# The first MLP's down projection in seven products, and the conditioning spread over TensorE and VectorE

## The chip, the cores and the metric

The kernel runs on one core of a Trainium2 chip: TensorE (PE) for matrix products, VectorE (DVE), ScalarE (ACT), GpSimd (POOL), and SyncE (SP), which issues all DMAs of this kernel in one queue. The metric is the device time of one execution in microseconds.

## The reference

One step of a two-layer encoder over 1024 prompt and 32 sample tokens, 1056 columns in the kernel. Everything is float32. What matters here:

```
D_MODEL = 1024; D_FF = 4096; DEPTH = 2
sh1, sc1, g1, sh2, sc2, g2 = split(silu(c) @ w_ada[l] + b_ada[l], 6)     # per layer, two conditions
kv_shift, kv_scale = split(silu(c) @ w_ada_kv + b_ada_kv, 2)
u = x * (1 + sc1) + sh1
y = mlstm(u) @ w_out_a            # layer 0;  layer 1: chunk-band attention @ w_out_b
x = layer_norm(ALPHA * x + (1 + g1) * y)
u = x * (1 + sc2) + sh2
f = square(relu(u @ w_up[l])) @ w_down[l]
x = layer_norm(ALPHA * x + (1 + g2) * f)
```

`c` has two rows, one for the prompt and one for the sample, so each conditioning vector is a product of a 1024 x 1024 matrix with two columns. Layer 0 needs six such vectors at the beginning. Layer 1 needs six and the shared K/V two, 64 column groups of 128.

## The kernel before

Activations lie transposed: 128 features on the partitions, tokens along the row. Tokens are cut into three blocks `TBS` of 384, 384 and 288, or into quarters `QN` of 264, two of which make a pair. For float32 accuracy each operand is split into a high and a low part (`split`: a cast on ACT and a subtraction on DVE), and each product is three matmuls, high x high, high x low and low x high (`proj`, L118 to L120). Weights come as 0.5 MB tiles (`wblock`): a DMA into one of three `raw` buffers, then a split into one of six `wc` buffers.

The order of the stages is: layer 0's conditioning and mixer, its output projection (`out_proj`, "op_a"), the first MLP, Q, K and V projections, attention, output projection ("op_b"), the second MLP, output.

A framework turns the program order into the order of each engine and places the waits. In between stands `Flow`: a generator such as a LayerNorm (`norm`) or the conditioning is added to it, each finished tile calls `flow.tick(us)`, and the generator goes on one step when the ticks that it asked for are used up. `flow.finish` issues the rest at once.

**First MLP, `mlp` (L1006).** 8 groups of 512 hidden features. `up(g, c, ti)` makes 128 of them for one block of tokens: 24 matmuls, relu and square on ACT, the split on DVE into `hs`. `down(g, w, fc, ...)` makes 12 matmuls for 128 outputs of one block and DVE adds them, times the gate, to the accumulator (`add_gated_at`, L986). Up of the next group alternates with down of this one. In the last group the blocks are finished one by one, with some up tiles between the first and the second, and `end0` starts the LayerNorm of each.

**Second MLP, `mlp7` (L1124).** Hidden features go in 16 blocks of 256. Up runs first, over everything. For the first 14 blocks (`NW`), four tiles (two halves of the features by two quarters) fill one `H` (3 buffers); ACT squares them, DVE forms sums and differences, and seven operands are split into `HL` (1 buffer) and stored to DRAM (`hd`, L1170). Blocks 14 and 15 are `up_plain`. Then down runs as a seven-product scheme (Strassen's, in Winograd's form): `forms` builds the seven weight operands from two raw tiles, `unit` does the seven products for one of 4 groups of blocks and one of 4 column groups, in an order of TensorE that is written out by hand, and `fill` brings the stored operands back into free `rooms`, among them the space of the inputs that up no longer needs. `step` and `prep` prepare the weights two units ahead. The two plain blocks follow as an ordinary product.

**Conditioning.** Layer 0's first two parts are done on TensorE at the start (`ada_mm`, L380): the condition is the weight operand, 32 columns wide, and the rows of the matrix stream through into a strip of 32 PSUM rows; four strips are used. All else is done on DVE (`ada_cols`, L225): for two column groups, 8 row blocks x 2 conditions of scalar times tile plus accumulator, 256 wide (L238, L241), then a transpose and a sum (L245, L246), and after four such pairs a small product on TensorE (L252). `ada_rest` (L1382) runs layer 1's 48 and the 16 column groups of K/V in this way beside the first MLP, starting at its third block, and `end0` finishes it before the last LayerNorms. Its tiles take turns with the weights in the three `raw` buffers.

Of the kernel before, what the change touches and what calls it, by code (L numbers as in the profile page):

```python
# [15 lines left out]
P = 128  # L16
# [59 lines left out]
def trunk_kernel(ctx: ExitStack, tc: tile.TileContext, a, o):  # L76
# [148 lines left out]
    def ada_cols(src, c0, base, nch, mk, tmp_f, step, raw_f=raw_tile):  # L225

        for j in range(0, nch, 2):
# [21 lines left out]
            if j // 2 % 4 == 3:  # L249
                ps = mk(f"adas_{base}_{j}")  # L250
                for q in range(4):
# [7 lines left out]
                    op=ALU.add)  # L259

# [539 lines left out]
    def open_acc(l, order, between=None):  # L800

        cms, accs = {}, {}
        for ti in reversed(order):
            cms[ti] = tc.tile_pool(name=f"acc{l}_{ti}", bufs=1, side="right", reuse_waits="tile")
            accs[ti] = cms[ti].__enter__().tile([P, KC, TBS[ti][1]], F32, name=f"acc{l}_{ti}")
        for ti in order if between is None else reversed(order):
            t0, n = TBS[ti]
            nc.sync.dma_start(accs[ti], xsp[l][:, :, t0:t0 + n])
            if between:
                between(ti)  # L810
        return cms, accs

    ADA_B = (4.0, 2.0, 1.0)
    NOW = True
    TAIL = (1.0, 1.5)
    W00 = (6.0, 12.0, 0.0, 0.0, 0.0, 3.0)
    W01 = (6.0, 12.0, 3.0, 3.0, 3.0)
    W10 = ((10.0, 12.0, 0.0, 0.0, 0.0, 3.0), (16.0, 14.0, 0.0, 0.0, 0.0, 3.0))
    EARLY = 2

    def make_layer(acc, pp, uo, cut=None):
# [184 lines left out]
        def mlp(hp, l, gate, order, before_tb, after_tb, last):  # L1006
            w_up, w_dn = a["w_up"][l], a["w_down"][l]
            NG = 8
            hs = {}
            wups = {}  # L1010

            def up_w(g, pr):
                if (g, pr) not in wups:
                    wups[g, pr] = [wblock(f"up{l}_{g}_{pr}_{i}", w_up, 512 * i, g * 512 + pr * 256) for i in range(2)]
                return wups[g, pr]

            def up(g, c, ti):
                t0, n = TBS[ti]
                ps = mm(f"up_{l}_{g}_{c}_{t0}")
                proj(ps[:, :n], n, up_w(g, c // 2), c % 2, lambda hl, k: uo(hl, k, t0, n))  # L1020
                if (g, c) not in hs:
                    hs[g, c] = hp.tile([P, 2, T], F32R, tag="h", name=f"h_{l}_{g}_{c}", bufs=5)
                ht = hs[g, c]
                r = tmp_t([P, 384], f"r_{l}_{g}_{c}_{t0}")[:, :n]
                nc.scalar.activation(r, ps[:, :n], AF.Relu)  # L1025
                nc.scalar.activation(ht[:, 0, t0:t0 + n], r, AF.Square)
                nc.vector.tensor_mul(r, r, r)
                nc.vector.tensor_sub(ht[:, 1, t0:t0 + n], r, ht[:, 0, t0:t0 + n].bitcast(F32))  # L1028
                flow.tick(n / 96)
# [769 lines left out]
```

## Time and profile before

| | us |
|---|---|
| median of 3 runs | 2479.54 (2476.41 to 2479.93) |
| profiled execution, device time | 2479.81 |
| its span, first to last instruction | 2478.0 |
| TensorE busy / VectorE busy / ScalarE busy | 2413.7 / 1759.7 / 1016.9 |
| first up matmul of the first MLP | 515.1 |
| first Q matmul | 1263.6 |
| first up matmul of the second MLP | 1732.2 |
| its first down matmul | 2110.2 |

The granted TensorE clock is 0.992 on average over the span. A row of the timeline has the start, the duration and the instruction; successive matmuls overlap, so their pace is the distance of their starts. A row of a group has the line, the engine, the operation, result and operands, shapes and count, then the busy time, the mean duration in ns, and the idle time before. A row of stages has the bounds, the length, then busy time and count of PE, weight loads, DVE, ACT and POOL, the clock, the DMA share and GB/s. In square brackets stands for how long an engine was idle before an instruction and what ended this.

### The profile page before, as it was taken

The numbers are of one execution on the slowest core, as the hardware profiler recorded it, in microseconds if no ns is written. First come the engines' busy times: TensorE is split into PE (matmuls) and PEld (weight loads), VectorE is DVE, ScalarE is ACT, GpSimd is POOL, SyncE is SP. The second block draws the span as 40 slices with busy tenths as digits, with TensorE's granted clock in tenths as the row PEclk, the third lists the DMA queues.
The fourth block names the chain that finished last, engine by engine and source line by source line (L and its number), as shares of the span: only waits on it lengthen the run. The fifth ranks groups of instructions, "written<-read, shape, count | busy, mean of one in ns | idle before, by whom it ended". The sixth has DMA issues, their size and how long they took to land.

```text
span 2478.0 us, 42688 instructions
## 1 busy us (share of the span) xinstructions
PE 2413.7 (97%) x16844; PEld 2315.4 (93%) x16844; DVE 1759.7 (71%) x4038; ACT 1016.9 (41%) x2118; POOL 168.6 (7%) x315
## 2 busy tenths in 40 slices
PE   7999999999999999999999999999999999999997
PEld 4999999999999999999999867789999999899997
DVE  4899999788679679677597667746853442776758
ACT  4644456382211212212266556654754443221212
POOL 0211100000000000000001134410000000000003
PEclk9999999999999999999999989999999999999999
DMA  8433224313224224234122310050375646767632
GB/s 297 122 110 101 84 88 129 107 35 119 77 87 137 84 86 135 80 92 142 43 98 82 91 40 1 18 147 27 134 251 212 215 179 254 262 239 273 255 130 72
DMA packets 236220, 318.10 MB, mean 128 GB/s; under 512 B 11624, under 2 KB 185084, under 8 KB 234996
## 3 DMA queue, kind: packets, MB, share of 16 engines
q1 hardware_dynamic: 236020, 315.38, 38.8%
q8 instruction: 132, 2.16, 0.4%
q14 instruction: 68, 0.56, 0.1%
HBM read 242.79 MB, written 74.91 MB: 128 GB/s over the span
## 4 chain that ended last, share of the span: by engine, by line
PE 78%; DVE 8%; DMA 6%; ACT 2%; issue 1%; POOL 0%; SPq 0%; DVEq 0%; POOLq 0%; ACTq 0%
PE up L118 10%; PE up L120 10%; PE up L119 9%; PE dn L1283 9%; PE dn L119 5%; PE dn L118 5%; PE dn L120 5%; DMA fx<-hd 3%; PE pv L1608 2%; PE pt L1588 2%; PE s L1558 2%; PE o L118 1%; PE o L119 1%; PE o L120 1%; PE op_b L118 1%
## 5 line engine op out<-in xcount | busy, mean ns | idle before, releaser
L120 PE MATMUL up<-u,w_up 128*128 128x264 f32 x1024 | 292.9, 286 | 0.0
L118 PE MATMUL up<-u,w_up 128*128 128x264 f32 x1024 | 292.4, 286 | 0.0
L119 PE MATMUL up<-u,w_up 128*128 128x264 f32 x1024 | 291.1, 284 | 0.0
L1283 PE MATMUL dn<-fx,wf 128*128 128x264 f32 x2208 | 275.3, 286 | 7.9 <-DMA fx<-hd 7.4
L1283 PEld LDWEIGHTS dn<-fx,wf 128*128 128x128 f32 x2208 | 272.2, 189 | 9.7 <-issue 4.6
L119 PE MATMUL dn<-h,w_dn 128*128 128x384 f32 (+1 forms) x768 | 249.5, 325 | 0.0
L118 PE MATMUL up<-U,w_up 128*128 128x384 f32 (+1 forms) x768 | 249.2, 324 | 0.0
L119 PE MATMUL up<-U,w_up 128*128 128x384 f32 (+1 forms) x768 | 247.9, 323 | 0.0
L118 PE MATMUL dn<-h,w_dn 128*128 128x384 f32 (+1 forms) x768 | 247.8, 323 | 0.0
L120 PE MATMUL up<-U,w_up 128*128 128x384 f32 (+1 forms) x768 | 247.6, 322 | 0.0
L120 PE MATMUL dn<-h,w_dn 128*128 128x384 f32 (+1 forms) x768 | 247.3, 322 | 0.0
L119 PEld LDWEIGHTS up<-u,w_up 128*128 128x128 f32 x1024 | 193.9, 189 | 0.0
L118 PEld LDWEIGHTS up<-u,w_up 128*128 128x128 f32 x1024 | 193.8, 189 | 0.0
L120 PEld LDWEIGHTS up<-u,w_up 128*128 128x128 f32 x1024 | 193.3, 189 | 0.0
L986 DVE SCALAR_TENSOR_TENSOR ACC<-dn,ada,ACC 128x264 f32<-128x264 f32 (+4 forms) x328 | 131.7, 426 | 86.4 <-PE dn L1283 74.6
L238 DVE SCALAR_TENSOR_TENSOR aacc<-rada,cs,aacc 128x256 f32<-128x256 f32 x448 | 190.3, 477 | 0.0
L986 DVE SCALAR_TENSOR_TENSOR acc<-dn,ada,acc 128x384 f32<-128x384 f32 (+2 forms) x256 | 119.4, 486 | 47.4 <-PE dn L120 46.3
L1025 ACT ACTIVATE r<-up 128x384 f32<-128x384 f32 (+1 forms) x96 | 44.3, 463 | 246.9 <-PE up L120 238.4
L119 PEld LDWEIGHTS dn<-h,w_dn 128*128 128x128 f32 x768 | 144.4, 188 | 0.2 <-DVE h L1028 0.2
L120 PEld LDWEIGHTS dn<-h,w_dn 128*128 128x128 f32 x768 | 144.5, 188 | 0.0
L120 PEld LDWEIGHTS up<-U,w_up 128*128 128x128 f32 x768 | 144.3, 188 | 0.0
L118 PEld LDWEIGHTS up<-U,w_up 128*128 128x128 f32 x768 | 144.2, 188 | 0.1
(354 smaller groups left out, 5957.4 us busy)
## 6 DMA issues: line engine op xcount, KB each, us to landing
hd<-HL SPq DMA_DIRECT2D x28, 1848.0 KB
raw_up<-in_w_up_dram SPq DMA_DIRECT2D x68, 512.0 KB
rada<-in_w_ada_dram SPq DMA_DIRECT2D x64, 512.0 KB
fx<-hd SPq DMA_DIRECT2D x37, 528.0 KB
raw_dn<-in_w_down_dram SPq DMA_DIRECT2D x36, 512.0 KB
ada_room<-in_w_ada_dram SPq DMA_DIRECT2D x32, 512.0 KB
fx<-hd SPq DMA_DIRECT2D x50, 264.0 KB
fx<-hd SPq DMA_DIRECT2D x16, 792.0 KB
```

What stands on the lines that cost most here:

```text
L118: nc.tensor.matmul(ps, wh, mov(0, k), start=(k == 0), stop=False)
L119: nc.tensor.matmul(ps, wh, mov(1, k), start=False, stop=False)
L120: nc.tensor.matmul(ps, wl, mov(0, k), start=False, stop=(k == nk - 1))
L238: nc.vector.scalar_tensor_tensor(acc[:, cnd], raw[:, k], sc, acc[:, cnd], op0=ALU.mult, op1=ALU.add)
L986: nc.vector.scalar_tensor_tensor(xs, ps[:, off + o:off + o + mm_], gate[:, fc, cnd:cnd + 1], xs, op0=ALU.mult, op1=ALU.add)
L1025: nc.scalar.activation(r, ps[:, :n], AF.Relu)
L1283: nc.tensor.matmul(p, ws[w][:, wl, k], t[:, s0, xl], start=first and k + n_ == 0, stop=k == kg - 1 and n_ == 2, skip_group_check=not first)
L1558: nc.tensor.matmul(s[:, b, :w], qst, kk[i][:, g, k0 + j0:k0 + j0 + w], start=(i == 0), stop=(i == 1))
L1588: nc.tensor.transpose(pt[:kp, j - j0, pr * P:(pr + 1) * P], ps_[pr][:, j * P:j * P + kp], ident)
L1608: nc.tensor.matmul(pv[64 * e:64 * e + 64, :nq], V[:kp, vt0 + j, g * 64:(g + 1) * 64], pts[e][:kp, j, :nq], start=(j == 0), stop=(j == nt - 1))
```

## The change

The first MLP uses `mlp7` as the second one does, by a class `L0`; `mlp` is gone. Its accumulator becomes one tile, `ACC0`, freed at once when Q's second block begins. Weights of the first three blocks of up are loaded during op_a.

The conditioning is done in four tasks. Beside the first MLP's up, `ada_up` takes turns: one step of `ada_rows` (two of layer 1's six parts, as whole rows on TensorE, as layer 0's first parts are), two steps of `ada_more` (four parts, 512 wide on DVE). Beside the first MLP's down, `ada_down` does a fifth part in 256-wide pieces; `ada_last` does the sixth beside the second MLP's up, from where its last LayerNorm is finished.

In `mlp7`, for both MLPs, the first unit's raw weights are loaded before the first fill, plain blocks use two buffers of their own, `forms` overwrites its raw tiles in place of two temporaries, and `prep` comes one product later.

```diff
+    def ada_more(parts, nb, mk, tmp_f, raw_f, step):
+        n = nb * P
+        todo = [(src, c0, base, j, k0) for src, c0, base, nch in parts for j in range(0, nch, nb) for k0 in range(0, KC, 2)]
...
+        for i, (_, _, base, j, k0) in enumerate(todo):
+            ahead = load(i + (1 if step else 0))
+            if not step:
+                raw = ahead
+            yield step[0][i % len(step[0])] if step else 0.0
...
+            for k in range(2):
+                for cnd in range(2):
+                    sc = cs[:, k0 + k, cnd:cnd + 1]
+                    if k0 + k:
+                        nc.vector.scalar_tensor_tensor(accs_[cnd], raw[:, k], sc, accs_[cnd], op0=ALU.mult, op1=ALU.add)
+                    else:
+                        nc.vector.tensor_scalar(accs_[cnd], raw[:, k], sc, None, op0=ALU.mult)
...
+            for cnd in range(2):
+                at = tmp_f([P, n], f"aat{cnd}_{base}_{j}")
+                nc.vector.transpose(at, accs_[cnd])
...
-    ADA_B = (4.0, 2.0, 1.0)
+    ADA_U, ADA_D, ADA_1 = 5.5, ((11.0,), 20.0), ((11.0,), 20.0)
-    W00 = (6.0, 12.0, 0.0, 0.0, 0.0, 3.0)
+    W00 = ((6.0, 12.0, 0.0, 0.0, 0.0, 3.0), (6.0, 12.0, 0.0, 0.0, 0.0, 3.0), (16.0, 14.0, 0.0, 0.0, 0.0, 3.0))
...
-                hl = hlp.tile([P, 2, 2, QN], F32R, tag="hl", name=name, bufs=2) if pb == NPB - 1 else \
-                    ring.tile([P, 2, 2, QN], F32R, tag="raw", name=name, bufs=3)
+                hl = hlp.tile([P, 2, 2, QN], F32R, tag="hl", name=f"hl{l}_{pb}_{f}_{tp}", bufs=2)
...
-            nc.vector.tensor_sub(s3, a11, a21)
-            nc.vector.tensor_sub(s4, a12, s2)
+            nc.vector.tensor_sub(a11, a11, a21)
+            nc.vector.tensor_sub(a12, a12, s2)
...
+        prep(0)
         for t in f4:
             rooms.add(t)
         want += [(tp, f) for tp in L.pairs for f in order_f]
         fill(0, fx)
         for tp in L.pairs:
-            up_plain(NW, tp)
-        prep(0)
-        up_plain(NW + 1, tp0)
+            up_plain(LP, tp)
         for _ in range(4):
             got[0] = next(preps[0])
         prep(1)
+        up_plain(LP + 1, tp0)
...
+    def ada_rows(src, c0, base):
+        acc = tmp_t([P, 256], f"arow_{base}")
+        for k in range(KC):
+            raw = raw_tile([P, D], f"rrow_{base}_{k}")
+            nc.sync.dma_start(raw, src[k * P:(k + 1) * P, c0:c0 + D])
+            yield
+            ps = mm(f"arow_{base}_{k}")[:, :256]
+            for q in range(4):
+                nc.tensor.matmul(ps[32 * q:32 * q + 32], cs[:, k, :], raw[:, q * 256:(q + 1) * 256],
+                                 start=True, stop=True)
+            if k:
+                nc.vector.tensor_add(acc, acc, ps)
+            else:
+                nc.vector.tensor_copy(acc, ps)
+        yield
+        ps2 = mm(f"arowt_{base}")[:, :256]
+        for b in range(2):
+            nc.tensor.transpose(ps2[:, b * P:(b + 1) * P], acc[:, b * P:(b + 1) * P], ident)
...
+    def ada_up():
+        def rows():
+            for i in range(2):
+                yield from ada_rows(a["w_ada"][1], i * D, 48 + 8 * i)
+        by_rows = rows()
+        by_cols = ada_more([(a["w_ada"][1], 2 * D, 64, 8), (a["w_ada_kv"], 0, 96, 16), (a["w_ada"][1], 3 * D, 72, 8)],
+                           4, mm, tmp_t, raw_tile, None)
+        live = [by_rows, by_cols, by_cols]
+        while live:
+            for g in list(live):
+                if g in live:
+                    if next(g, live) is live:
+                        live = [x for x in live if x is not g]
+                    else:
+                        yield ADA_U
...
+    def ada_down():
+        yield from ada_more([(a["w_ada"][1], 4 * D, 80, 8)], 2, mm, tmp_t, tmp_t, ADA_D)
...
+    def ada_last():
+        yield from ada_more([(a["w_ada"][1], 5 * D, 88, 8)], 4, mm, tmp_t, raw_tile, ADA_1)
...
-    mlp(hp, 0, ada_part(0, 5), fwd, before0, end0, TBS)
+    class L0:
+        l, alloc, add, gate, wups = 0, mm, add_gated_at, ada_part(0, 5), wup0
+        pairs, quarters, blocks = (0, 1), (0, 1, 2, 3), TBS
+        ready, after = before0, end0
...
+    mlp7(L0)
...
             if gi == 0:
                 flow.finish(norms[ti])
-                acc_cm[ti].__exit__(None, None, None)
+                if ti == 1:
+                    flow.finish(norms[2])
+                    acc_cm0.__exit__(None, None, None)
```

206 lines of the change are left out of this document (98 added, 108 removed).

## The prediction

> **What bounds the kernel now.** I read the page's first part, then the busy time by stage, then the timeline of TensorE inside the two MLPs.
>
> ```profile
> PE 2413.7 (97%) x16844; PEld 2315.4 (93%) x16844; DVE 1759.7 (71%) x4038; ACT 1016.9 (41%) x2118; POOL 168.6 (7%) x315
> ```
>
> TensorE is busy in 97% of the span. So an edit pays if it removes matmul time, and costs if it makes TensorE wait. The stages below are, in order: the whole first MLP (first up matmul to first Q matmul); the second MLP's up until its last LayerNorm block is ready; the rest of up; its two plain blocks of up; the first 30 us of its down; the rest of that down; the plain remainder.
>
> ```profile
> core 0: us, PE busy (x) PEld busy (x) DVE busy (x) ACT busy (x) POOL busy (x), PEclk, DMA share, GB/s
> 515.10:1263.70 748.60, 748.51 (x4685) 746.14 (x4684) 556.46 (x1195) 204.16 (x354) 0.00 (x0) 1.00 0.30 93
> 1732.20:1785.00 52.80, 52.55 (x415) 52.34 (x415) 49.50 (x86) 41.93 (x75) 0.00 (x0) 0.97 0.40 132
> 1785.00:2063.00 278.00, 278.00 (x2280) 278.00 (x2279) 122.03 (x152) 130.76 (x199) 0.00 (x0) 1.00 0.60 212
> 2063.00:2110.20 47.20, 47.20 (x389) 47.20 (x388) 14.92 (x24) 21.40 (x41) 0.00 (x0) 1.00 0.74 265
> 2110.20:2140.00 29.80, 24.01 (x171) 22.73 (x170) 18.14 (x42) 7.89 (x17) 0.00 (x0) 0.89 1.00 384
> 2140.00:2408.80 268.80, 266.70 (x2186) 266.12 (x2185) 189.59 (x418) 55.18 (x98) 0.00 (x0) 1.00 0.59 211
> 2408.80:2463.70 54.90, 53.54 (x442) 52.98 (x440) 41.23 (x108) 12.74 (x28) 18.02 (x13) 1.00 0.28 105
> ```
>
> The second MLP already works in seven products, so these rows are the pattern for the first one. Busy time of pipelined matmuls overlaps; what counts is the distance from start to start. On the timeline of the first MLP (start, duration, instruction):
>
> ```profile
> 807.16 0.34 PE L118 MATMUL up<-U,w_up 128*128 128x384 f32 x1
> ...
> 815.58 0.29 PE L118 MATMUL up<-U,w_up 128*128 128x288 f32 x1
> ...
> 818.77 0.34 PE L118 MATMUL up<-U,w_up 128*128 128x384 f32 x1
> ```
>
> Here 48 matmuls of 384 columns take 8.42 us (0.1754 each) and 24 of 288 take 3.19 (0.1329), so one weight over all 1056 columns costs 2 x 0.1754 + 0.1329 = 0.4837 us. The chain of the seven products gives the same for 264 columns:
>
> ```profile
> 2201.58 73.31 PE dn L1283 x600
> ```
>
> Less one tail of 0.28, 599 distances take 73.03 us: 0.1219 each, four of them 0.4876 us. Narrower blocks cost almost nothing by themselves.
>
> **The matmuls of the first MLP.** Before: up and down are each 32 x 8 weights by 3 split terms, 1536 rounds of 1056 columns: 1536 x 0.4837 = 743.0 us. It took 748.6, so 5.6 us are stalls and the eight small conditioning products. After: up is 3072 x 0.1219 = 374.5; seven products x 14 blocks x 4 column groups x 2 pairs x 3 terms = 2352 matmuls, 286.7; the two plain blocks 96 x 0.4837 = 46.4. Together 707.6, so at most 41 us are to be won against 748.6.
>
> The second MLP shows what such code takes in fact. Up ran from 1732.2 to 2110.2: 378.0, which is 3.5 over its matmuls. Down ran from 2110.2 to 2408.8: 298.6, 11.9 over. Half of that is the first window of down: 24.01 us busy of 29.80 at a clock of 0.89 with the DMA engines full, since the stored halves of H must come back before a product can start:
>
> ```profile
> 2127.49 2.32 PE L1283 MATMUL dn<-fx,wf 128*128 128x264 f32 x9 [3.15 <-DMA fx<-hd]
> ```
>
> Copied to the first MLP this gives 378.0 + 298.6 + 46.4 = 723.0, or **-25.6 us**. From here on come the additions.
>
> **Conditioning on TensorE.** Two of the six parts go as whole rows: 2 x 8 steps of four fp32 matmuls, 256 columns wide, into four 32-row strips. No row shows this form. The nearest are a 257-column fp32 product with full weights and a 128-column fp32 transpose, then the small strip products of today's conditioning, then strip products of 512 columns at the start:
>
> ```profile
> 200.15 0.59 PE L634 MATMUL cu<-vt,kw 128*128 128x257 f32 x2
> 200.58 0.38 PE L668 MATMUL hT<-ident,hn 128*128 128x128 f32 x2
> 200.80 0.39 PE L612 MATMUL S<-y,y 128*128 128x128 f32 x2
> ```
>
> ```profile
> 707.54 0.29 PE L120 MATMUL dn<-h,w_dn 128*128 128x288 f32 x1
> 707.76 0.26 PE L252 MATMUL adas<-cx,sel 128*32 128x16 f32 x8
> 707.96 0.44 PE L118 MATMUL dn<-h,w_dn 128*128 128x384 f32 x1
> ```
>
> ```profile
> 25.78 1.06 PE L383 MATMUL ada<-rada,cs 128*32 128x512 f32 x8
> ```
>
> One fp32 product of 257 columns takes 0.43 us. Four of 512 one after the other would take 3.4; they are over in 1.06, so strips run side by side. A visit to strips and back costs 0.42 - 0.13 = 0.29 beyond the matmul before it. I take 0.43 + 0.29 = 0.72 a step: 16 x 0.72 = 11.5, plus four transposes of 0.22: 12.4, minus two small products of 0.29 that go: **+11.8 us**. In series a step would be 4 x 0.43 + 0.29 = 2.01, 20.6 us more in all. It cannot be under 0.43 a step, 4.6 less.
>
> The Trainium skill, TensorEngine Tiling (Array Packing), Key Properties, speaks against mixing these: changing the tiling mode drains TensorE. By an estimate from it, each step pays two drains of 0.28 - 0.12 = 0.16, so 0.75 a step and 0.5 us more in all; the trace's 0.29 for such a visit agrees, and I keep that.
>
> **Conditioning on VectorE beside up.** Today 64 columns are done in 256-wide pieces along the whole first MLP:
>
> ```profile
> L238 DVE SCALAR_TENSOR_TENSOR aacc<-rada,cs,aacc 128x256 f32<-128x256 f32 x448 | 190.3, 477 | 0.0
> ...
> L555 DVE SCALAR_TENSOR_TENSOR y<-qkp,pt,y 128x1059 f32<-128x1059 f32 x24 | 31.9, 1330 | 0.0
> ...
> L245 DVE STREAM_TRANSPOSE aat<-aacc 128x512 f32<-128x512 f32 x32 | 22.6, 706 | 0.3
> L630 PE MATMUL num<-vt,sT 128*128 128x257 f32 (+1 forms) x72 | 22.0, 387 | 0.0
> L246 DVE TENSOR_REDUCE cx<-aat 128x16 f32<-128x512 f32 x32 | 21.7, 679 | 0.2
> ```
>
> The line through 256 columns (477 ns) and 1059 (1330) gives 1.06 ns a column and 205 ns an instruction, so 749 ns for 512. A group of four columns is 16 such pieces and two transposes with sums of 1.385: 14.8 us (the opening two pieces are cheaper, which I ignore). Beside up stand 8 groups, 118 us, and 16 row sums of at most 0.48, 8 us: 126 us. The schedule has 51 steps of two up tiles, 24 matmuls each: 51 x 2 x 24 x 0.1219 = 298 us of the 316 left after the last LayerNorm, so little is left over for the point where it is forced to finish. VectorE carries 122.03 of 278 us there in the second MLP, 44%; with 126 of 298 it is 86%. It stays under TensorE, so the work itself is hidden; what it delays is the next point.
>
> **The loop through HL.** HL, the split copy of H that is stored to DRAM, has one buffer. Its cycle is cast (ACT), subtraction (DVE), store, and only then the next cast:
>
> ```profile
> 1937.45 1.83 ACT L89 CAST HL<-H 128x264 fp32r<-128x264 f32 x2 [1.31 <-DMA hd<-HL]
> ...
> 1949.30 1.83 ACT L89 CAST HL<-H 128x264 fp32r<-128x264 f32 x2 [1.62 <-DMA hd<-HL]
> ```
>
> ```profile
> 1926.00 1.81 DVE L90 TENSOR_TENSOR HL<-H,HL 128x1584 fp32r<-128x1584 f32 x1 [0.16 <-ACT HL L89]
> ...
> 1939.32 1.81 DVE L90 TENSOR_TENSOR HL<-H,HL 128x1584 fp32r<-128x1584 f32 x1 [0.17 <-ACT HL L89]
> ```
>
> Cast start to subtraction end is 1941.13 - 1937.45 = 3.7; the store then blocks the next cast for 1949.30 - 1941.13 = 8.2, so the loop is 11.9. TensorE needs 96 x 0.1219 = 11.7 for the four tiles that fill an H: the two are level already. With two weight loads ahead in SP's queue the store took 1937.45 - 1927.81 = 9.6. The change puts two more loads in each cycle:
>
> ```profile
> hd<-HL SPq DMA_DIRECT2D x28, 1848.0 KB
> raw_up<-in_w_up_dram SPq DMA_DIRECT2D x68, 512.0 KB
> rada<-in_w_ada_dram SPq DMA_DIRECT2D x64, 512.0 KB
> ```
>
> The windows move 212 GB/s at a share of 0.60; 48 loads of 0.52 MB in 298 us add 84 GB/s, about 0.84 in all. They fit, mostly into the 3.7 us in which no store runs. I charge the loop 0.3 us for a load ahead of the store and 0.8 for one VectorE piece in progress: 13.0 against 11.7 + 0.4 (row products) = 12.1 on TensorE, over 23 remaining cycles 21 us; H's three buffers absorb one cycle, 11.7. About half of the remainder of 9 should vanish where the loop is faster than shown: **+5 us** (bounds 0 and 33, below).
>
> **Smaller terms.** Beside down, a third conditioning task of 64 x 0.477 + 4 x 1.385 = 36 us lifts VectorE from 189.59 of 268.8 (71%) to 84%: +2, between 0 and 8. The last blocks of the first MLP lose the up tiles that stood between them, so its final LayerNorms have less time before the Q matmuls: +2, between 0 and 8. Weights of the first seven-product unit are now prepared before the fills, and plain blocks no longer take the raw buffers: -3 in each MLP, between 0 and -9, out of the 11.9 above. The last conditioning part moves beside the second MLP's up, 2 x 14.8 = 30 us of VectorE where it is 44% busy: +1, 0 to 6. Each of these is my choice between nothing and a stall of the size seen at the start of down.
>
> **Costed at nothing.** Up weights of three blocks are loaded during the output projection's last block, where two blocks' were before; the matmuls of that block hide them. The accumulator is one tile now, so the second third of Q's results waits until the last LayerNorm is stored. Today that norm ends long after the first Q matmul at 1263.7:
>
> ```profile
> L896 DVE TENSOR_TENSOR acc<-acc,w_n x24: 749/948/959, 481.3 to 1309.6; 128x768 f32<-128x768 f32 x16, 128x576 f32<-128x576 f32 x8
> ```
>
> That is 46 us after it, and the store comes on top, some 50. Q's first third takes 6 x 24 x 0.1754 = 25 us; the next 8 groups of 4.2 us fill the PSUM banks until 59. So ACT's copies wait, with weight casts behind them, but TensorE does not; without the banks it would lose 50 - 29 = 21 us. Delays of the last block's norm (16 and 14 ticks instead of 6 and 12) are covered by the 20 up tiles before it is needed.
>
> **Sum.** First MLP: 723.0 + 11.8 + 5 + 2 + 2 - 3 = 740.8, which is -7.8 against 748.6; second MLP -3 + 1 = -2. So -9.8 on the profiled execution's 2479.81 (span 2478.0 and 1.8 around it; the median 2479.54 is the same within 0.3): **2470 us**. A change under 0.2%, 5 us, cannot be told from none here.
>
> **Rivals.**
> 1. *The loop through HL becomes the bound (slower).* Its place is up of the first MLP, its price: cast to subtraction 3.7, a store with loads ahead each time 9.6, one VectorE piece 0.75: 14.05 a cycle. (14.05 - 12.1) x 23 - 11.7 = 33 us instead of 5: 2498. It decides from 12.6 us a cycle on, where 23 excesses fill the spare buffer. For it: loop and TensorE are level today, VectorE goes to 86%. Against: DMA has room for all the bytes, and the casts waited little. 0.17, spread over 2486 to 2510.
> 2. *Row products run in series:* 20.6 more, 2490.6. The x8 row speaks against it: 0.04.
> 3. *The gain is eaten at the seams:* the start of down keeps its whole stall in both MLPs (no -3) and the four small terms cost twice: 2470 + 6 + 5 = 2481, between 2475 and 2484. 0.19.
> 4. *All is covered:* none of the four small waits or the 5 arises (-10), and the start of down recovers 3 more in one MLP: 2457, between 2448 and 2463. For it: 278 of 278 us busy in the second MLP's up. 0.24.
>
> The forecast itself, 2463 to 2474.6, has 0.36. Faster: 0.36 + 0.24 = 0.60; same 0.19; slower 0.17 + 0.04 = 0.21. Cases of both signs matter; the forecast's own range is 2463 to 2475. The range for 8 in 10 leaves out the ends of rivals 1 and 4: 2450 to 2495.
>
> **What would show it.** Right: the first MLP shorter by about 8 us, from its first up matmul to the first Q matmul; up near 395 us with row products about 0.7 us apart from their neighbours; store to store near 12 us; down near 298; the same rows of the second MLP within 3 us. Wrong: waits of the relu copies or the up matmuls on HL's subtraction or on the store; a TensorE clock under 1 in up; strip products over 1.5 us a step; Q matmuls waiting for the last LayerNorm.

## The result, and the profile after

The changed kernel takes 2531.23 us (median of 4 runs, 2530.12 to 2535.38) against 2479.66 (4 runs of the kernel before on the same chip). The ratio is 1.0216, with a 95% interval from 1.0201 to 1.0231: **slower by 2%**. The forecast was 2470.0, the range ended at 2495. The views below are of the profiled execution, the longest of the four (2535.38).

TensorE's row in the page's first part, then the busy time by stage: first MLP's up, the first 30 us of its down, the rest of its down, its plain remainder; then the same of the second MLP without a remainder of its own.

```profile
PE 2419.4 (96%) x18064; PEld 2305.8 (91%) x18064; DVE 1779.8 (70%) x3930; ACT 1099.0 (43%) x2242; POOL 166.6 (7%) x315
```

```profile
core 0: us, PE busy (x) PEld busy (x) DVE busy (x) ACT busy (x) POOL busy (x), PEclk, DMA share, GB/s
513.70:946.40 432.70, 400.60 (x3242) 386.73 (x3241) 278.39 (x437) 204.85 (x337) 0.00 (x0) 0.96 0.71 241
946.40:976.40 30.00, 26.37 (x210) 25.46 (x208) 19.62 (x48) 6.67 (x13) 0.00 (x0) 1.00 0.92 326
976.40:1260.20 283.80, 270.29 (x2154) 267.67 (x2154) 216.77 (x500) 56.33 (x99) 0.00 (x0) 0.98 0.63 222
1260.20:1307.80 47.60, 47.60 (x297) 47.60 (x296) 34.97 (x57) 13.63 (x20) 0.00 (x0) 1.00 0.26 92
1779.90:2158.10 378.20, 377.95 (x3086) 377.56 (x3085) 210.48 (x305) 194.46 (x316) 0.00 (x0) 1.00 0.62 218
2158.10:2188.10 30.00, 24.36 (x156) 23.23 (x155) 15.46 (x36) 6.29 (x13) 0.00 (x0) 0.77 1.02 372
```

The two rows to set against each other are the first and the fifth: the same 3072 up matmuls take 378.2 us in the second MLP and 432.7 in the first. TensorE is idle there for 432.7 - 400.6 = 32 us, VectorE is busy only 64% of the time, and the DMA share is 0.71. Neither is full; something arrives late. The span grew by 2533.3 - 2478.0 = 55.3 us, of which the first MLP (first up matmul to first Q matmul) has 794.1 - 748.5 = 45.6, the second MLP's down 305.0 - 298.7 = 6.3, and the Q projection 3.9.

What TensorE waits for in that up, in the view of waits for this stretch (engine and line, what it waited for, us in total, times, longest):

```profile
ACT HL L89 <- DMA hd<-HL: 24.2, 15, 4.1
PE up L118 <- ACT w_up L89: 22.2, 8, 7.2
...
DVE aacc L293 <- DMA rada<-in_w_ada_dram: 12.1, 2, 9.3
...
PEld adas L310 <- DVE cx L304: 9.8, 1, 9.8
PE adas L310 <- DVE cx L304: 9.6, 1, 9.6
```

Of TensorE's 32 us, 22.2 are waits for the **up weights** (L89 is their cast) and 9.6 are one wait of the conditioning's small product, which stands in TensorE's order and waits for VectorE, which waits for its own loads. For H it hardly waits. Why the weights come late stands in SyncE's own waits in this stretch. L96 issues the loads of up weights, and these stood until a conditioning piece (`aacc`) or a row product (`arow`) had given back the buffer that they need:

```profile
SPq L96 <- DVE aacc L293: 22.7, 12, 3.4
...
SPq L96 <- PE arow L1379: 13.3, 5, 6.2
```

HL has a part in it: the two longest weight waits, 7.2 and 6.4 us, end with a weight cast that stands in ACT's order right behind a cast of HL. The first of them on the timelines of ACT and of TensorE, and what follows it in short windows:

```profile
797.84 1.82 ACT L89 CAST HL<-H 128x264 fp32r<-128x264 f32 x2 [2.89 <-DMA hd<-HL]
799.57 2.21 ACT L89 CAST w_up<-raw_up 128x1024 fp32r<-128x1024 f32 x2
```

```profile
800.66 0.59 PE L118 MATMUL up<-U,w_up 128*128 128x264 f32 x1 [7.25 <-ACT w_up L89]
801.05 0.42 PE L119 MATMUL up<-U,w_up 128*128 128x264 f32 x1
801.27 0.42 PE L118 MATMUL up<-U,w_up 128*128 128x264 f32 x1
```

```profile
793.40:800.66 7.26, 0.01 (x1) 0.00 (x0) 2.97 (x5) 4.24 (x5) 0.00 (x0) 0.79 0.94 301
800.66:804.66 4.00, 4.00 (x18) 3.79 (x19) 3.11 (x3) 1.05 (x1) 0.00 (x0) 0.53 0.56 211
804.66:808.66 4.00, 4.00 (x36) 4.00 (x34) 0.00 (x0) 0.39 (x1) 0.00 (x0) 1.00 1.00 285
```

A wait has a second price: after 7.25 us of idleness the granted clock is 0.53 for 4 us, matmuls start 0.22 us apart in place of 0.12, and 18 fit where 36 should. A wait of 7.25 us so costs about 9.

### The profile page after: what moved, and what is told of

Its sections match the earlier page's. It is cut to its first block, busy times and chain, and to the rows that moved or that the text cites. A ratio compares the mean times of both kernels' runs of the same rounds, so it can differ in the third digit from the quotient of the medians.

```text
span 2533.3 us, 45556 instructions
## 1 busy us (share of the span) xinstructions
PE 2419.4 (96%) x18064; PEld 2305.8 (91%) x18064; DVE 1779.8 (70%) x3930; ACT 1099.0 (43%) x2242; POOL 166.6 (7%) x315
## 4 chain that ended last, share of the span: by engine, by line
PE 69%; DVE 12%; DMA 10%; ACT 3%; issue 2%; POOL 0%; SPq 0%; ACTq 0%; DVEq 0%; POOLq 0%
PE dn L1254 20%; PE up L118 7%; PE up L120 7%; PE up L119 7%; PE pv L1665 2%; PE pt L1645 2%; DMA fx<-hd 2%; PE s L1615 2%; DMA hd<-HL 2%; DMA rada<-in_w_ada_kv_dram 1%; DMA raw_up<-in_w_up_dram 1%; DVE aacc L293 1%; PE o L118 1%; PE o L119 1%; PE o L120 1%
## 5 line engine op out<-in xcount | busy, mean ns | idle before, releaser
L1254 PE MATMUL dn<-fx,wf 128*128 128x264 f32 x3108 | 407.3, 288 | 16.4 <-DMA fx<-hd 7.0
L1254 PEld LDWEIGHTS dn<-fx,wf 128*128 128x128 f32 x3108 | 394.5, 192 | 18.9 <-issue 9.6
L1038 DVE SCALAR_TENSOR_TENSOR ACC<-dn,ada,ACC 128x264 f32<-128x264 f32 (+5 forms) x648 | 261.8, 429 | 179.9 <-PE dn L1254 154.6
L118 PE MATMUL up<-U,w_up 128*128 128x264 f32 x1024 | 296.6, 291 | 22.3 <-ACT w_up L89 22.2
L119 PE MATMUL up<-U,w_up 128*128 128x264 f32 x1024 | 293.2, 288 | 0.0
L120 PE MATMUL up<-U,w_up 128*128 128x264 f32 x1024 | 286.2, 286 | 0.2 <-DVE w_up L90 0.2
L89 ACT CAST wf<-rdn 128x384 fp32r<-128x384 f32 (+1 forms) x160 | 84.5, 565 | 327.3 <-PE dn L1254 158.3
L118 PEld LDWEIGHTS up<-U,w_up 128*128 128x128 f32 x1024 | 196.3, 192 | 29.9 <-ACT w_up L89 24.8
L119 PEld LDWEIGHTS up<-U,w_up 128*128 128x128 f32 x1024 | 196.3, 192 | 0.8 <-issue 0.8
L120 PEld LDWEIGHTS up<-U,w_up 128*128 128x128 f32 x1024 | 192.4, 191 | 2.3 <-DVE w_up L90 1.9
L1254 PE MATMUL dn<-U,wf 128*128 128x264 f32 x1308 | 178.8, 288 | 8.2 <-DMA U<-hd 4.2
L1254 PEld LDWEIGHTS dn<-U,wf 128*128 128x128 f32 x1308 | 168.4, 191 | 10.6 <-DVE ACC L1038 6.2
L90 DVE TENSOR_TENSOR HL<-H,HL 128x264 fp32r<-128x264 f32 x112 | 125.1, 1117 | 62.2 <-ACT HL L89 61.6
L293 DVE SCALAR_TENSOR_TENSOR aacc<-rada,cs,aacc 128x512 f32<-128x512 f32 (+1 forms) x196 | 121.9, 667 | 24.7 <-DMA rada<-in_w_ada_dram 14.6
L90 DVE TENSOR_TENSOR w_up<-raw_up,w_up 128x1024 fp32r<-128x1024 f32 x72 | 87.3, 1219 | 61.6 <-ACT w_up L89 61.4
```

What stands on the lines that cost most here:

```text
L89: nc.scalar.copy(dst_h, src)
L90: (eng or nc.vector).tensor_sub(dst_l, src, dst_h.bitcast(F32))
L118: nc.tensor.matmul(ps, wh, mov(0, k), start=(k == 0), stop=False)
L119: nc.tensor.matmul(ps, wh, mov(1, k), start=False, stop=False)
L120: nc.tensor.matmul(ps, wl, mov(0, k), start=False, stop=(k == nk - 1))
L293: nc.vector.scalar_tensor_tensor(accs_[cnd], raw[:, k], sc, accs_[cnd], op0=ALU.mult, op1=ALU.add)
```

## The experiments

Thirteen kernels ran. Stages are measured from start to start: "up" from the first to the last up matmul, "down" on to the first matmul with the plain halves `hs`, "plain" on to the first Q matmul.

| run | up 1 | down 1 | plain 1 | Q | down 2 | time | before, same chip |
|---|---|---|---|---|---|---|---|
| before | (first MLP: 748.5 in all) | | | 95.8 | 298.7 | 2479.81 | |
| after | 432.7 | 313.8 | 47.6 | 99.7 | 305.0 | 2531.23 | 2479.66 |
| e1_none | 375.2 | 318.8 | 47.5 | 97.9 | 301.2 | 2476.70 | 2476.92 |
| e2_noload | 388.1 | 310.6 | 47.5 | 99.8 | 304.5 | 2488.60 | 2476.92 |
| e3_loadonly | 407.9 | 312.3 | 47.5 | 99.8 | 302.4 | 2508.48 | 2476.92 |
| e4_room | 409.4 | 314.0 | 47.5 | 98.5 | 305.7 | 2511.43 | 2476.92 |
| e8_small | 398.8 | 315.9 | 48.0 | 98.5 | 303.9 | 2501.70 | 2478.01 |
| e9_queue | 447.6 | 312.9 | 47.5 | 98.5 | 303.3 | 2547.01 | 2478.01 |
| e5_edits | | | | 95.8 | 307.3 | 2487.59 | 2478.01 |
| e6_nodown | 433.8 | 298.0 | 47.6 | 98.2 | 305.5 | 2521.74 | 2478.01 |
| e7_prep | 424.0 | 312.4 | 47.5 | 99.6 | 298.4 | 2514.86 | 2478.12 |
| e10_downnoload | 431.8 | 299.4 | 47.6 | 99.8 | 305.3 | 2518.56 | 2478.12 |
| e12_sum | 406.6 | 308.4 | 47.5 | 121.6 | 301.0 | 2521.66 | 2478.12 |
| e13_rooms | 405.7 | 314.0 | 47.5 | 98.4 | 300.2 | 2507.53 | 2478.67 |
| e14_neither | 375.2 | 313.2 | 47.5 | 100.7 | 305.9 | 2479.15 | 2478.67 |

Times of the changed kernel, e12 and e13 are medians of 4 runs, and their stages are those of the profiled execution (2535.38, the longest of its four; 2520.47; 2503.13, the shortest of its four). The other experiments ran once each. Stages that are the same code in several kernels show how well they repeat: up 1 takes 431.8 to 433.8 in the changed kernel, e6 and e10.

### What makes up slow: products, VectorE, or loads

Three kernels take the conditioning beside the first MLP's up apart.

e1_none, none of it:

```diff
-        by_rows = rows()
-        by_cols = ada_more([...], 4, mm, tmp_t, raw_tile, None)
-        live = [by_rows, by_cols, by_cols]
+        nc.vector.tensor_copy(ada[:, 48:80, :], pt2[:, 48:80, None].broadcast_to([P, 32, 2]))
+        nc.vector.tensor_copy(ada[:, 96:112, :], pt2[:, 96:112, None].broadcast_to([P, 16, 2]))
+        yield ADA_U
+        live = []
```

> Leaves out the conditioning products beside the first MLP's up (layer 1's first four parts and the K/V pair get their bias only): no loads, no VectorE pieces, no row products there. Up of the first MLP took 432.8 us in the changed kernel (513.7 to 946.5), the second MLP's 378. All three theories that blame the conditioning expect 378 to 384, so a total near 2480. A theory that blames the seven-product up itself, with the first layer's data or buffers, expects over 410.

e2_noload, all of its instructions, without its loads:

```diff
-            raw = raw_tile([P, D], f"rrow_{base}_{k}")
-            nc.sync.dma_start(raw, src[k * P:(k + 1) * P, c0:c0 + D])
+            raw = U[:, :D].bitcast(F32)
...
+            if not step:
+                return U[:, :D].bitcast(F32).rearrange("p (k c) -> p k c", k=2)
```

> All conditioning work beside the first up stays, 128 wide pieces and 64 row products, but its operands are read from the up inputs already in SBUF, so the 48 loads of 0.5 MB are gone (wrong values, same work). Theory VectorE (its 3 us bursts delay H's and the weights' splits): up stays near 430. Theory raw buffers (conditioning and weights share three, so weights come late) and theory DMA volume (stores of HL and loads compete): up falls to 390 to 398, which is 378 plus 12 for the row products.

e3_loadonly, all loads and row products, but slivers of 16 columns in place of most VectorE pieces:

```diff
-                    if k0 + k:
+                    if k0 + k and not step:
+                        if cnd:
+                            nc.vector.scalar_tensor_tensor(accs_[cnd][:, :16], raw[:, k, :16], sc, accs_[cnd][:, :16],
+                                                           op0=ALU.mult, op1=ALU.add)
+                    elif k0 + k:
                         nc.vector.scalar_tensor_tensor(accs_[cnd], raw[:, k], sc, accs_[cnd], op0=ALU.mult, op1=ALU.add)
```

> The opposite: all 48 loads and the row products stay, but of the column pieces beside up only the two opening ones per group are whole, the other 14 shrink to 7 of 16 columns, and the transposes and sums go. VectorE work there falls from about 120 us to about 15. Theory VectorE: up falls to 390 to 400. Theory raw buffers: smaller effect, since a buffer is still held until its step comes; 415 to 433. Theory DMA volume: 425 to 433.

Without conditioning up takes 375.2, near its bare matmuls of 374.5. All instructions without loads add 388.1 - 375.2 = **12.9 us**, which is the row products on TensorE; VectorE's pieces are hidden (it is busy 278.39 us in the changed kernel's up and 171.80 in that of e14_neither, so about 107 us). TensorE has no idle time at all in e2's up:

```profile
517.30:905.40 388.10, 388.10 (x3242) 378.53 (x3241) 275.80 (x437) 202.21 (x337) 0.00 (x0) 1.00 0.58 204
```

The loads add the rest, 432.7 - 388.1 = **44.6 us**: 32.1 us in which TensorE is idle, and 400.6 - 388.1 = 12.5 by which it is busy longer with the same matmuls, at a granted clock of 0.96 against 1.00. With the loads but hardly any VectorE work up takes 407.9, a time that none of the three theories gave. So the loads alone cost 407.9 - 388.1 = 19.8, and another 24.8 come with the whole pieces, which cost nothing without loads. That they do it by holding the buffers longer fits this, but e3 does not separate it from VectorE's time.

### Bytes, buffers or queue

e4_room gives the conditioning loads a buffer of their own (one of six `wc` buffers), so that they leave the three `raw` ones to the weights:

```diff
-            raw = raw_tile([P, D], f"rrow_{base}_{k}")
+            raw = room(k)
...
+        rm = [ring.tile([P, 2112], F32, tag="wc", name=f"ada_room{i}", bufs=6) for i in range(1)]
...
-                           4, mm, tmp_t, raw_tile, None)
+                           4, mm, tmp_t, room_c, None)
```

> The full work with the same loads, but the conditioning beside up has buffers of its own: one of the six buffers of split weights is taken for it, half for rows, half for columns, and the three raw buffers are left to the weights. Right results. Theory raw buffers: up 390 to 400 and a total near 2495. Theory DMA volume and theory VectorE: no change, up 425 to 435; with five buffers for weights it may even be longer.

e8_small keeps every load, its buffer and its use, but loads 32 columns only and computes on resident data:

```diff
-            nc.sync.dma_start(raw, src[k * P:(k + 1) * P, c0:c0 + D])
+            nc.sync.dma_start(raw[:, :32], src[k * P:(k + 1) * P, c0:c0 + 32])
...
+            nc.vector.tensor_add(acc[:, :32], acc[:, :32], small[:, :32])
```

> The 48 loads beside the first up stay, in the same queue, into the same shared raw buffers and held as long, but each brings 32 columns of a row instead of 1024 or 512; the pieces and row products read the up inputs instead, and one small addition reads the loaded part (wrong values, same work). Up took 432.7 us with the loads and 388.1 without. Theory bytes (the 25 MB compete with weights and HL stores): near 390. Theory buffers (weights wait for one of three raw buffers, and SP stands still behind that wait): 415 to 433.

e9_queue issues the same loads from GpSimd's queue:

```diff
-            nc.sync.dma_start(raw, src[k * P:(k + 1) * P, c0:c0 + D])
+            nc.gpsimd.dma_start(raw, src[k * P:(k + 1) * P, c0:c0 + D])
```

> Full work and right results; only the 48 loads are issued by GpSimd, idle in this stage, so that a load waiting for a buffer no longer holds up the weight loads and HL stores behind it in SP's queue. Theory SP's order: up near 400. Theory buffers alone or bytes alone: 425 to 435, since both stay.

None of the three came out within the ranges of its theories. Small loads in the shared buffers cost 398.8 - 388.1 = 10.7 us over none, full loads in a buffer of their own 409.4 - 388.1 = 21.3, and full loads in the shared buffers 44.6; so 12.6 arise only where both meet. A buffer of their own takes 432.7 - 409.4 = 23.3 away, full bytes and all. What the other 21.3 are stands in e4's trace, in its up and in the waits there:

```profile
516.90:926.30 409.40, 394.22 (x3242) 384.40 (x3241) 278.44 (x436) 201.16 (x337) 0.00 (x0) 0.97 0.74 251
```

```profile
PE adas L310 <- DVE cx L304: 14.6, 3, 8.2
```

TensorE is idle for 15.2 us and waits for no up weights any more. 14.6 of these are three waits of the small product for the conditioning's columns; the other 6.1 of the 21.3 are matmuls at a lower clock. So the sharing is what made the weights late, and what remains is conditioning that is late for its own place in TensorE's order. With one room for columns, e4's loads of columns have to wait for the piece before them (51.8 us in 24 of SyncE's waits); how much of the delay is this and how much the bytes was not isolated. Another queue did not help: issued by GpSimd, the same loads made up 14.9 us longer, with 29.2 us of waits for weights and one of 9.9 for a row product's load.

### The part beside down

e6_nodown leaves `ada_down`'s product out; e10_downnoload keeps its VectorE instructions and leaves out its loads and their temporaries:

```diff
-        yield from ada_more([(a["w_ada"][1], 4 * D, 80, 8)], 2, mm, tmp_t, tmp_t, ADA_D)
+        nc.vector.tensor_copy(ada[:, 80:88, :], pt2[:, 80:88, None].broadcast_to([P, 8, 2]))
+        yield 5.0
```

> Leaves out the conditioning product beside the first MLP's down (that part gets its bias only). The first down took 313.8 us, the second MLP's before the change 298.7. Theory VectorE beside down: 300 to 305. Rival, the seam (stored operands come back late) and the changed preparation of weights: 311 to 314; the run without conditioning beside up had 318.8.

```diff
+            if nb == 2:
+                return cs.rearrange("p k c -> p (k c)")[:, None, :].broadcast_to([P, 2, n])
             raw = raw_f([P, 2, n], f"rada_{base}_{j}_{k0}")
```

> The changed kernel, with the conditioning part beside the first MLP's down reading a constant that is already on the chip: its 16 loads and their temporary buffers are left out (that sixth of the conditioning is not the reference's), its VectorE instructions are all still there. Without that part altogether down took 298.0 us, with it 313.8. Theory VectorE (the 36 us of pieces delay the sums in the seven products): down stays near 312. Theory buffers and loads (five temporaries shared with the weight sums, each held until its load has landed and been used): down falls to 298 to 301.

The part costs 313.8 - 298.0 = 15.8 us in down, and 14.4 of them (313.8 - 299.4) go with its loads and temporaries, though all VectorE pieces stay. Waits of the weight casts, of the changed kernel's down and then of e10's (whose lines stand two later):

```profile
ACT wf L89 <- DVE s L1216: 39.9, 8, 16.0
...
ACT wf L89 <- DVE s L1217: 20.7, 7, 17.7
```

```profile
ACT wf L89 <- DVE s L1218: 17.0, 6, 4.4
...
ACT wf L89 <- DVE s L1219: 4.6, 8, 1.3
```

Casts waited 60.6 us for the two sums `s1` and `s2` and wait 21.6 here. Sums and conditioning take turns in five temporaries; a load in use, the next one ahead and an accumulator held over four loads leave few for the sums. (e6's 298.0 alone would have fitted VectorE as well, whose theory had 300 to 305; e10 decides.)

### The edits in `mlp7`

e5_edits is the kernel before with only the edits of `mlp7` that both MLPs share. e7_prep is the changed kernel with the order of preparation put back:

```diff
-        prep(0)
         for t in f4:
...
+        prep(0)
+        up_plain(LP + 1, tp0)
         for _ in range(4):
             got[0] = next(preps[0])
         prep(1)
-        up_plain(LP + 1, tp0)
...
-                    if j == 4:
+                    if j == 3:
```

> The kernel before with only the edits inside the seven-product function, so they act on the second MLP alone: weights of the first unit loaded before the fills, later units one product later, no temporaries, own buffers for plain blocks. My prediction had this 3 us shorter: down of the second MLP 295.7 against 298.7. The changed kernel and its variants show 301 to 306 there. If the edits do it, 302 to 306 here; if the sixth conditioning part beside that up does it, 298.7.

> The changed kernel, with one thing undone in both MLPs: the weights of the first seven-product unit are prepared after the fills again and the plain blocks' work stands where it stood in the kernel before. The sums written in place and the plain blocks' own buffers stay. Theory A (the order of preparation is what lengthens the second MLP's down): that down takes 299 us, as before, and the first MLP's some 6 less than 313.8. Theory B (the in-place sums or the buffers are): the second MLP's down stays at 304 to 307. In both, up of the first MLP stays at 432 and the span is 2520 to 2534.

The edits alone lengthen the second MLP's down by 307.3 - 298.7 = 8.6 us, and putting the order back in the changed kernel gives 298.4: the order is the cause, and the in-place sums and the plain blocks' own buffers cost nothing there. The size is less sure, since the second down takes 301.2 to 307.3 in the runs with the new order and 298.4 to 301.0 in those with the old one. Which of the two moves does it, the first unit earlier or the later units one product later, was not separated. The first 30 us of the second MLP's down, windows of 10 us, of the changed kernel and then of e7_prep:

```profile
2158.10:2168.10 10.00, 8.27 (x67) 7.88 (x65) 8.04 (x20) 3.31 (x7) 0.00 (x0) 1.00 0.99 350
2168.10:2178.10 10.00, 6.39 (x31) 5.92 (x32) 2.50 (x5) 0.93 (x2) 0.00 (x0) 0.58 1.02 377
2178.10:2188.10 10.00, 9.70 (x61) 9.43 (x61) 4.92 (x11) 2.05 (x4) 0.00 (x0) 0.74 1.05 389
```

```profile
2144.70:2154.70 10.00, 9.53 (x75) 9.03 (x73) 8.98 (x23) 3.54 (x7) 0.00 (x0) 1.00 1.02 362
2154.70:2164.70 10.00, 5.07 (x27) 4.35 (x27) 2.35 (x5) 0.93 (x2) 0.00 (x0) 0.90 1.02 394
2164.70:2174.70 10.00, 9.12 (x67) 8.59 (x67) 6.25 (x14) 2.56 (x5) 0.00 (x0) 0.93 1.05 389
```

TensorE is idle for about as long, 5.6 and 6.3 us, and the DMAs are full in both. The clock differs: 0.58 and 0.74 against 0.90 and 0.93. But this is worth little: 159 matmuls start in the changed kernel's 30 us and 169 in e7's, and ten of them are 1.2 of the 305.0 - 298.4 = 6.6 us. The rest is lost later. What follows these 30 us, to the plain remainder, in the changed kernel and in e7, and the longest of the changed kernel's waits there:

```profile
2188.10:2463.10 275.00, 270.34 (x2202) 269.61 (x2201) 192.02 (x423) 55.63 (x99) 0.00 (x0) 0.99 0.57 208
```

```profile
2174.70:2443.10 268.40, 267.08 (x2189) 266.54 (x2188) 190.75 (x419) 55.53 (x98) 0.00 (x0) 1.00 0.59 211
```

```profile
2250.36 8.35 PE L1254 MATMUL dn<-fx,wf 128*128 128x264 f32 x54 [1.78 <-ACT wf L89]
```

TensorE is idle there for 4.7 us against 1.3, and its longest wait, 1.78 us, is for a cast of weights: with the new order weights come late at a later turn. The low clock of the first 30 us on the timeline of the changed kernel:

```profile
2168.05 1.33 PE L1254 MATMUL dn<-fx,wf 128*128 128x264 f32 x9 [1.72 <-DMA fx<-hd]
2171.28 4.30 PE L1254 MATMUL dn<-fx,wf 128*128 128x264 f32 x18 [1.89 <-DMA fx<-hd]
2177.29 2.32 PE L1254 MATMUL dn<-fx,wf 128*128 128x264 f32 x9 [1.72 <-DMA fx<-hd]
```

Eighteen matmuls take 4.30 us, half speed, between waits under 2 us. The Trainium skill, TensorE: Matmul & The Clock Gate, HAM oscillation, describes such re-throttling from DMA waits, and gives idle gaps over about 3.4 us as its rule. The half speed agrees with the rows; the listed gaps here are shorter.

In the first MLP the order works both ways. e7's up is 432.7 - 424.0 = 8.7 us shorter, and 7.7 of these are idle time: e7 lacks the 9.6 us wait of the small product, whose last load of columns SyncE issues 12.7 us after the last store of a half in e7 and 26.6 us after it in the changed kernel. But e7's down starts worse (189 matmuls in its first 40 us against 264, rows in the next section) and ends at 312.4 against 313.8, not some 6 us shorter as theory A had it. In all, the new order costs 794.1 - 784.0 = 10.1 us in the first MLP.

### Do the costs add

e12_sum takes three costs out at once: a buffer of their own for the loads beside up, the old order of preparation, and the part beside down moved beside the Q projection. e13_rooms leaves that part beside down and gives its loads a `wc` buffer too. e14_neither leaves out all conditioning beside the first MLP.

```diff
+        rm = ring.tile([P, 2112], F32, tag="wc", name="ada_room0", bufs=6)
...
-            norms["ada"] = flow.add(ada_down())
...
     mlp7(L0)
+    norms["ada"] = flow.add(ada_down())
```

> The changed kernel with three of the found costs taken out together: the conditioning loads beside up have a buffer of their own for rows and one for columns (measured alone: up 409.4 in place of 432.7), the part beside down goes beside the Q projection (measured alone: 15.8 less in down, and whatever it costs there), and the first unit's weights are prepared in the order of the kernel before. If the costs add, the first MLP takes 409 + 298 + 47.5 = 755 us and the span is 2533.3 - 23 - 16 - 0 to 12 + 0 to 8 beside Q, 2482 to 2502: between the two kernels, still not faster than before. If up and down only pass one cost on to each other, the span stays over 2510.

```diff
-        yield from ada_more([(a["w_ada"][1], 4 * D, 80, 8)], 2, mm, tmp_t, tmp_t, ADA_D)
+        rd = ring.tile([P, 4, 2, 256], F32, tag="wc", name="ada_room1", bufs=6)
...
+        yield from ada_more([(a["w_ada"][1], 4 * D, 80, 8)], 2, mm, tmp_t, room_d, ADA_D)
```

> The changed kernel with buffers of their own for the conditioning loads beside up and beside down (one of the six weight buffers each, at different times), and the first unit's weights prepared in the order of the kernel before. If the three costs found one by one are separate (shared buffers beside up 23, temporaries beside down 14, order of preparation 7 in the second MLP), the first MLP takes 406 + 300 + 47.5 = 754 us, the second MLP's down 299, and the span is 2533 - 23 - 14 - 7 to 10 = 2486 to 2490, still some 10 us over the kernel before. If the start of the first MLP's down is what loses 9 us in place of them, as where the part was moved beside Q, it is 2495 to 2505.

For e14_neither, the edits of e1_none and e6_nodown together.

> The changed kernel without any conditioning beside the first MLP's up or down (those five sixths of it and the key part are not the reference's). If the copied pattern of the second MLP holds and the costs add, up is 375, down 298, the plain remainder 47.5: 721 us, and the span 2533.3 - 73 = 2460. If the first MLP's down has a cost of its own that the part beside it only shares, down stays over 305 and the MLP over 728.

They don't add. e12's span of 2518.7 lies over the 2482 to 2502 of the sum, and over the 2510 that stood for costs passed on from up to down (ratio to before 1.0179, interval 1.0162 to 1.0196): beside Q the part costs 121.6 - 99.7 = 22, more than beside down. e13 is the fastest form of the changed kernel that leaves nothing out, 2507.53 (2503.13 to 2511.36), ratio 1.0117 (1.0100 to 1.0134), still slower than before; the span of its profiled run, 2501.3, is the case named for a start of down that loses. And **e14, with nothing beside up and down, has a down of 313.2**, as long as the changed kernel's. The first 40 us of the first MLP's down in e14, then in e6_nodown, e2_noload, the changed kernel and e7_prep:

```profile
888.70:928.70 40.00, 25.95 (x159) 24.21 (x158) 18.87 (x40) 9.21 (x18) 0.00 (x0) 0.74 0.97 346
```

```profile
949.20:989.20 40.00, 36.44 (x291) 35.38 (x289) 24.65 (x60) 8.11 (x17) 0.00 (x0) 1.00 0.82 275
```

```profile
905.40:945.40 40.00, 35.28 (x282) 34.30 (x281) 29.66 (x74) 9.04 (x18) 0.00 (x0) 1.00 0.96 332
```

```profile
946.40:986.40 40.00, 34.61 (x264) 33.63 (x263) 27.86 (x69) 8.77 (x18) 0.00 (x0) 0.96 0.94 328
```

```profile
937.80:977.80 40.00, 29.12 (x189) 28.07 (x188) 17.88 (x43) 6.35 (x13) 0.00 (x0) 0.83 0.94 326
```

TensorE has 159 matmuls there in e14 and 291 in e6; at 0.122 us each the difference is 16 us, which is all of 313.2 - 298.0 = 15.2. On the timeline of e14 it waits for halves of H, which were stored during up and must be back before down can start:

```profile
901.89 0.88 PE L1254 MATMUL dn<-U,wf 128*128 128x264 f32 x3 [3.00 <-DMA U<-hd]
...
910.10 4.30 PE L1254 MATMUL dn<-U,wf 128*128 128x264 f32 x18 [2.59 <-DMA U<-hd]
```

A fast up is not by itself the reason. e2's up has no idle time either, and its down, with the conditioning part beside it, begins with 99 matmuls without a wait for a transfer:

```profile
905.50 6.00 PE L1256 MATMUL dn<-fx,wf 128*128 128x264 f32 x48
911.34 6.38 PE L1256 MATMUL dn<-U,wf 128*128 128x264 f32 x51
```

What sets e14 and e1 apart lies at the beginning of up. In these two the third store comes 32.1 us after the second; in the other eleven kernels that have the new first MLP it is 11.2 or 11.3. SyncE's and ACT's rows of e14:

```profile
556.89 0.37 SPq L1143 DMA_DIRECT2D hd<-HL  x1
557.30 29.75 SPq L96 DMA_DIRECT2D raw_up<-in_w_up_dram  x3
589.00 0.37 SPq L1143 DMA_DIRECT2D hd<-HL  x1
```

```profile
582.90 1.05 ACT L89 CAST w_up<-raw_up 128x1024 fp32r<-128x1024 f32 x1 [7.48 <-PE up L120]
...
585.31 1.82 ACT L89 CAST HL<-H 128x264 fp32r<-128x264 f32 x2
```

Two weight casts, which wait for TensorE to give back their buffers, stand before the third cast of HL in ACT's order; in e2 they stand behind it. The third store so starts 75.5 us after up's first matmul in e14 and 54.6 in e2. The last one starts 28.0 us after the matmuls of the 14 stored blocks have ended in e14, and 6.9 in e2. Both times e14 is 21 us later, so the delay is never made up, and down meets it. Why the order differs when the conditioning's work is missing was not traced, and no run takes this delay out alone. But e14's 735.9 us are not the pattern's own time: they hold a delay that the changed kernel does not have. The times named for a cost of down's own (over 305 and 728) came out, but this delay is enough for them.

A late store is also not the only way to lose the start of down. e7, e12 and e13, with the old order of preparation, lose it too, though their last store stands 43.5, 38.7 and 38.8 us before the end of up. In e13 down's start waits 9.2 us for halves in `U`, which stand in SyncE's queue behind two stores of plain halves; what would free that start was not tried.

## Why the prediction was wrong, point by point

**The first MLP's pattern, copied: 723.0, with +2 at the end and -3 for the order.** Up was right (375.2 for 378.0, without conditioning) and so was the remainder (47.5 for 46.4). Down was right where nothing stood beside it and its halves were on time: 298.0 for 298.6 in e6. Together these are 720.7, but no run shows them together. e14 was to, and took 735.9 with its late halves, so that what a run shows of the pattern's gain is 748.5 - 735.9 = 12.6 us; with the second MLP's loss e14's time, 2479.15, is that of before, 2478.67.

**Row products +11.8:** 12.9 measured. Strips run side by side, as I took it:

```profile
789.46 0.28 PE L120 MATMUL up<-U,w_up 128*128 128x264 f32 x1
789.67 0.64 PE L1379 MATMUL arow<-rrow,cs 128*32 128x256 f32 x8
790.24 0.39 PE L118 MATMUL up<-U,w_up 128*128 128x264 f32 x1
```

From 789.46 to 790.24 are 0.78 us, less 0.12 for the matmul before it: 0.66 for a step priced 0.72 (each of its four products leaves two records). The two drains that I took from the Trainium skill, TensorEngine Tiling (Array Packing), Key Properties, would give 0.75 by that estimate; this row shows less. Rival 2, a series of 2.01, is out.

**Loads and VectorE beside up, +5 with bounds 0 and 33: the step that failed.** It is 44.6. I counted queue positions (0.3 us a load) and bytes (0.84 of the DMAs in all, so "they fit") and charged both to the loop through HL. The share did stay below, 0.71. But two waits stand in none of my terms. The 48 loads went into the three `raw` buffers through which every up weight passes, so weights came late, and TensorE waited 22.2 us for them; with a buffer for the loads (e4) it waits for none. And the small product, which I counted by its 0.29 us alone, waits in TensorE's order for its columns: 9.6 us here, 14.6 in e4. At the lower clock TensorE is busy 12.5 us longer on top. The row products' loads I costed as matmuls alone.

**Rival 1, the loop through HL becomes the bound, 2498:** right sign, too small, and its mechanism is a part at most. TensorE hardly waits for HL or H, and H's three buffers were not what ran out; what ACT waits for the stores reaches TensorE only through weight casts that stand behind it, as at 800.66.

**Beside down, +2 (0 to 8):** 15.8 in e6, of which 14.4 go with loads and temporaries and not with VectorE's pieces. In e1 and e14, where the start of down waits anyway, the same part costs 318.8 - 313.2 = 5.6.

**Edits in `mlp7`, -3 in each MLP (0 to -9):** +6.6 in the second and +10.1 in the first. I expected weights to be late at the start of down. In the second MLP the halves of H are late there with either order, and with the new one weights are late further on. In the first MLP the start of down does gain, but up pays for it by the wait of the small product.

**Q's wait for the last LayerNorm, +2 and nothing for TensorE:** the Q stage is 3.9 longer, inside the 0 to 8 that I gave. **The last part beside the second MLP's up, +1:** 378.2 against 377.9, right.

**The sum.** The first MLP was to take 740.8 and took 794.1. Of the 53.3 missing, up has 432.7 - (378.0 + 11.8 + 5) = 37.9, down 313.8 - (298.6 + 2 - 3) = 16.2 and the remainder 47.6 - (46.4 + 2) = -0.8. Rivals 3 and 4 moved the same small terms by a few us and so could not reach this.

## What to carry to other kernels

Before placing loads "beside" a TensorE stage because engines and DMAs have room, count the buffers: which tiles do they pass through, who else takes turns there, and for how long does each use hold one. Ask also what the work beside it puts into the busy engine's own order: a small product there waits for its data like a large one, and everything behind it waits too. Take the costs out one at a time and all together, because only the second shows which of them hide one another. And read in the trace whether the rest stayed as it was: leaving work out also moves what is left, as the third store of e14, and then the difference is not the price of what was left out.

## What the hardware showed that I had not expected

A wait costs TensorE more than its length. After 7.25 us idle the clock was 0.53 for 4 us, and between waits of 1.7 to 1.9 us 18 matmuls ran at half speed. How long TensorE is idle does not decide alone: of two stretches of 30 us with 5.6 and 6.3 us of idle time, the clock was 0.58 and 0.74 in windows of the one and 0.90 and 0.93 in the other. What decides was not settled. And a second queue was no relief: the same 48 loads issued by GpSimd in place of SyncE lengthened up from 432.7 to 447.6 us.
